# Attention's edge units scaled block by block, the next mLSTM head's decay made within the present head, fillers moved

## The chip, the cores and the metric

One Trainium2 chip, of which the program uses one core. The metric is device time in microseconds (us) of one execution, and the median of three executions is given. Names of engines: PE multiplies matrices (PEld loads its weights), DVE is the vector engine, ACT the scalar engine with the table functions, POOL the general engine (GpSimd), SP issues most DMA transfers.

## The reference

One decoder layer on 512 tokens of width 1024. A normalized input goes through one wide projection; two branches follow, an mLSTM matrix memory (4 heads of 256) and a sparse attention (8 query heads of 64 in 2 groups, with a compressed, a selected and a window part); gates merge them, and an output projection, the residual and a last norm follow. Cut to what is touched:

```python
hN = _rmsnorm(x, norm_g[l])
p = _split_in(hN @ w_in[l])
# mLSTM, one chunk: gates as cumulated decays, then a normalized product
logD = a[..., :, None] - a[..., None, :] + li[..., None, :]
m_t = jnp.maximum(inter, jnp.max(logD, axis=-1))
s = jnp.einsum('bhld,bhsd->bhls', qc, kc) * jnp.exp(logD - m_t[..., None])
h = num / jnp.maximum(jnp.abs(den), jnp.exp(-m_t))[..., None]
mh = _head_layernorm(mh, mh_norm_g[l]).astype(x.dtype)
# attention: softmax parts, each weighted by a gate per head and token
p_s = jax.nn.softmax(s_s, axis=-1)
p_w = jax.nn.softmax(jnp.where(m_w, s_w, NEG), axis=-1)
return g[..., 0:1] * o_c + g[..., 1:2] * o_s + g[..., 2:3] * o_w
# end
x = x + merged @ w_out[l]
return _rmsnorm(x, final_norm_g)
```

With 512 tokens in 8 selectable blocks of 64 and a window of 512, the selected and the window part both see every earlier token.

## The kernel before

Every large product is done in float32 by three passes: each operand is split into a high part (rounded) and a low rest, and high by high, high by low and low by high are added in PSUM. The split of a weight tile `wr` (128 x 1024) is one ACT copy to `wh` and one DVE subtraction to `wl`.

**Fillers.** The projection's columns, 128 at a time, are jobs of a `Stream` (line 164). `stream.step(n)` issues n of its matmuls (128 x 512, `pp<-hTh,wh` and the like) into the program; when a job is through, its `post` function evacuates it. The kernel places such steps by hand, by constants, between the parts of attention and of the mLSTM heads, so that PE has work while another engine prepares what it needs next. PE keeps the order that a scheduler makes of the program by its dependencies; ACT and DVE keep program order only while their name is in the set `ordered` (lines 68 to 82).

**Attention** consists of 16 units `(c, hh, b)`: four query pairs, two halves, two branches (selected and window). A unit has four query blocks `qb` of 128 rows, the causal part of each being 128, 256, 384 or 512 columns wide, all in one tile `P` (128 x 1280). `score` (line 1033) makes the scores of a block into PSUM `ps` (two buffers, tag `ps`), `softmax_block` (line 1024) takes the row's minimum of the negated scores with a custom DVE instruction (`P,st<-ps,cst`) and the exponential with its row sum on ACT. At the last block the reciprocals of the four sums and the gates are multiplied on DVE (`st`), and four POOL instructions (line 1055) scale P. `ptrans` (line 1057) then transposes P by PE (`pt<-cst,P`), and the products with the values follow (`po<-pth,vsw`). Scores run a unit ahead of the values. `tick` (line 1090) issues FILL = 3 filler steps between these pieces, in the last quarter two; between the four scores of the first unit it is START_FILL = 12. The compressed part (`sc`, `mx`, `pc`) runs beside it as a generator. Before attention stand the keys (`keys`), the compressed keys and values (`compress_k` writes `KC`, `compress_v` writes `VC`) and the first queries (`query_heads`, which turns them by position, `rope_b`, and splits them into `Th`); 4 and 14 filler steps lie between them (lines 967 to 972).

**mLSTM.** For each of four heads (loop at line 1255): the decay matrix `Dm` (a PE product of `sel` and `ghl` in PSUM, `dg` on DVE, seven exponentials on ACT), four score blocks times Dm, four value products into `num` with statistics (`bs`, `mv`) on DVE, then `rho` (the normalizer) and, over the power on POOL (`rlr`), the scale of each row, by which `num` is multiplied, on DVE for two of four blocks and on ACT for two. Transposes of num follow (`pt<-cst,num`). Each head's queries and keys (`qkh`, `qkl`) come from convolutions (`conv`, line 1178: three DVE steps `u<-pp,prm,u`, a tanh and a split) that are the `post` of filler jobs; before the transposes the loop steps the stream until the next head's last convolution is through (line 1324), in the last head NORM_FILL = 30 steps.

**Tail.** The last norm of row blocks 0 and 1: `more` and `factor` (lines 1457 and 1461) add up partial sums of squares `fb` and take the power `fr` on POOL, `last_factor` reduces the last piece by a custom DVE instruction, `times` and `both` multiply by the norm's weights, `scaled` multiplies by `fr` on ACT and stores.

Of the kernel before, what the change touches and what calls it, by code (L numbers as in the profile page):

```python
# [15 lines left out]
OP = mybir.AluOpType  # L16
# [4 lines left out]
NT = T // 128  # L21
ND = D // 128
# [1 line left out]
BIG = 1e30  # L24
NEGINF = -3.0e38
FILL = 3
START_FILL = 12
LAG = 1
BEHIND = 2
YIELDS = 6  # L30
NORM_FILL = 30

MQ, MK, MV, MO, MZ, MI = 0, 1024, 2048, 3072, 4096, 5120
NQ, NKC, NVC, NKS, NVS, NKW, NVW = 5128, 5640, 5768, 5896, 6024, 6152, 6280
# [26 lines left out]
def build(  # L61
# [5 lines left out]
    ordered = {"act", "dve"}  # L67
# [809 lines left out]

        cols(NQ + c * 128, post)

    def query_heads(c):  # L880
        raw, rot, a = roped.pop(("q", c))
        q = rope_b(raw, rot, a)
        Th = []
        for hh in range(2):
            s = slice(hh * 64, hh * 64 + 64)
            o = slice((1 - hh) * 64, (1 - hh) * 64 + 64)
            t = rpp.tile([128, T], F32R, name="Th", tag=f"Th{hh}")
            A(t[s, :], q[s, :], AF.Copy)
            dve.tensor_tensor(t[o, :], q[s, :], f(t[s, :]), OP.subtract)
            Th.append(t)  # L890
        heads[c] = raw, Th
# [71 lines left out]
    stream.run()  # L963
    keys(0, rope_b(*roped.pop(("k", 0))))
    u1 = hidden(1)
    stream.run()
    keys(1, rope_b(*roped.pop(("k", 1))))
    stream.step(4)
    ordered.update(("act", "dve"))
    query_heads(0)  # L970
    compress_k(u0)
    stream.step(14)
    compress_v(u1)
    ordered.clear()
    cmp_pool.__exit__(None, None, None)

# [47 lines left out]
    def softmax_block(c, hh, b, qb, pss, P, st):  # L1024
# [5 lines left out]
        )  # L1030
        A(pv, pv, AF.Exp, bias=st[:, 0, qb : qb + 1], scale=-1.0, accum_out=st[:, 1, qb : qb + 1])

    def score(c, hh, b, qb, pair):
        kh, kl = KK[c // 2]
        n = (qb + 1) * 128
        tq = heads[c][1][hh][:, qb * 128 : qb * 128 + 128]
        if qb == 0:
            if b == 0:
                pss = PS()
                pe.matmul(pss[:, :256], tq, kh[:, :, :128], start=True, stop=False)  # L1040
                pe.matmul(pss[:, :256], tq, kl[:, :, :128], start=False, stop=True)
                for i in range(2):
                    softmax_block(c, hh, i, 0, pss[:, i * 128 : i * 128 + 128], *pair[i])
            return
        pss = PS()
        pe.matmul(pss[:, :n], tq, kh[:, b, :n], start=True, stop=False)
        pe.matmul(pss[:, :n], tq, kl[:, b, :n], start=False, stop=True)
        P, st = pair[b]
        softmax_block(c, hh, b, qb, pss[:, :n], P, st)
        if qb == NT - 1:  # L1050
            dve.reciprocal(st[:, 2], st[:, 1])
            dve.tensor_tensor(st[:, 2], st[:, 2], gates[:, :, (2 * c + hh) * 3 + 1 + b], OP.mult)
            for j in range(NT):
                pj = P[:, POFF[j] : POFF[j] + (j + 1) * 128]
                pool.tensor_scalar(pj, pj, st[:, 2, j : j + 1], 1.0, OP.mult, OP.mult)  # L1055
# [187 lines left out]

        stream.add(load, gen)

    for h in range(4):
        for i in range(2):
            for e in range(2):
                conv(i, h, e)
    for j in range(ND):  # L1250
        branch(GB, j, ybh, ybl, 4)
    stream.run(4)
    values(0)

    for h in range(4):
        (qh, ql), (kh, kl) = qk[0, h], qk[1, h]
        vh, vl = vv[h]
        pgb = PS()
        sl = sel[:, h : h + 1].broadcast_to([128, 128])
        pe.matmul(pgb, sl, ghl, start=True, stop=True)  # L1260
# [6 lines left out]
        for sb in range(NT):  # L1267
            o, n = KOFF[sb], 512 - sb * 128
            bias = cs[:, sb, h : h + 1]
            A(Dm[:, o : o + 128], dg[:, sb * 128 : sb * 128 + 128], AF.Exp, bias=bias, scale=-1.0)  # L1270
            if n > 128:
                A(Dm[:, o + 128 : o + n], pgb[:, (sb + 1) * 128 :], AF.Exp, bias=bias, scale=-1.0)
        Sh = mp.tile([128, 1280], F32R, name="Sh", tag="Sh")
        Sl = mp.tile([128, 1280], F32R, name="Sl", tag="Sl")
        for sb in range(NT):
# [14 lines left out]
        for tb in range(NT):  # L1290
            po = PO() if tb == 2 else PT()
            for sb in range(tb + 1):
                a = KOFF[sb] + (tb - sb) * 128
                lh, ll = Sh[:, a : a + 128], Sl[:, a : a + 128]
                pe.matmul(po[:, :258], lh, vh[:, sb, :], start=sb == 0, stop=False)
                pe.matmul(po[:, :256], lh, vl[:, sb, :], start=False, stop=False)
                pe.matmul(po[:, :258], ll, vh[:, sb, :], start=False, stop=sb == tb)
            A(num[:, tb], po[:, :258], AF.Copy)
            dve.bn_stats(bs[:, tb], num[:, tb, 0:256])
            dve.bn_aggr(mv[:, tb], bs[:, tb])  # L1300
# [21 lines left out]
        if h < 3:  # L1322
            values(h + 1)
            while (1, h + 1, 1) not in ready:
                stream.step(1)
        else:
            stream.step(NORM_FILL)
        for e in range(2):
# [15 lines left out]
    with tc.tile_pool(name="fin", bufs=1, reuse_waits="tile") as fp:  # L1344
# [109 lines left out]
        def begin(tb):  # L1454
            keep(pool.tensor_scalar(fb[:, tb : tb + 1], fs[:, tb, 0:1], EPS, None, OP.add))

        def more(tb, n):
            v = fb[:, tb : tb + 1]
            keep(pool.tensor_tensor(v, v, fs[:, tb, n : n + 1], OP.add))

        def factor(tb, n):
            more(tb, n)
            keep(pool.tensor_tensor(fr[:, tb : tb + 1], fb[:, tb : tb + 1], mhalf[:, 0:1], OP.pow))  # L1463

        def last_factor(tb, cs, n):
# [96 lines left out]
        product((None, Y[1]), "MS4", w3, False, tbs=(1,), cs=halves_of[0])  # L1562
        join(1, R0, Y[1][:, halves_of[0]])
        square(1, R0, 1)
        times(0, R)
        factor(0, 1)
        more(1, 1)
        scaled(0, L)
        scaled(0, R)
        product((None, Y[2]), "MS4", w3, False, tbs=(1,), cs=halves_of[1])  # L1570
# [27 lines left out]
```

## Time and profile before

| | us |
|---|---|
| median of 3 runs (lowest to highest) | 612.02 (611.96 to 612.77) |
| the profiled execution | 612.24 |
| its span, from first to last instruction | 610.4 |

The granted clock is 0.997. What is quoted from the profile further on has these forms. A row of the page's first part is an engine's busy time, its share of the span and the count of its instructions. A wait row names engine and tile that waited, the engine and tile that released it, then total us, times and longest. A row of stretches is "start:end length", then the busy time and count of PE, PEld, DVE, ACT and POOL, the granted clock, the DMA share and GB/s. A timeline row is start, duration, engine, line, operation, output and inputs with shapes, count, and in brackets the idle time ahead of it and what ended it. A row of groups is line, engine, operation, tiles, shapes and count, then the summed time in us and the mean in ns, then idle time. L77 is the line of the helper that records most instructions, so the tiles tell them apart.

### The profile page before, as it was taken

The numbers are of one execution on the slowest core, as the hardware profiler recorded it, in microseconds if no ns is written. First come the engines' busy times: TensorE is split into PE (matmuls) and PEld (weight loads), VectorE is DVE, ScalarE is ACT, GpSimd is POOL, SyncE is SP. The second block draws the span as 40 slices with busy tenths as digits, with TensorE's granted clock in tenths as the row PEclk, the third lists the DMA queues.
The fourth block names the chain that finished last, engine by engine and source line by source line (L and its number), as shares of the span: only waits on it lengthen the run. The fifth ranks groups of instructions, "written<-read, shape, count | busy, mean of one in ns | idle before, by whom it ended". The sixth has DMA issues, their size and how long they took to land. (4 is left out here: it accounts for less than half of the span.)

```text
span 610.4 us, 8577 instructions
## 1 busy us (share of the span) xinstructions
PE 596.2 (98%) x3008; PEld 499.5 (82%) x3008; DVE 483.1 (79%) x906; ACT 343.2 (56%) x635; POOL 63.4 (10%) x126
## 2 busy tenths in 40 slices
PE   8999999999999999999999999999999999999995
PEld 6988888888888877888888887888788878888884
DVE  5879798696686578886977684889898997589984
ACT  6854646664442356665765674465756563434564
POOL 3000000000100003222122131000000000010122
PEclk9999999999999999999999999999999999999998
DMA  7966555302068361323313113422242234890633
GB/s 221 349 162 190 183 168 160 116 2 86 18 185 207 78 173 46 97 59 86 81 47 103 53 34 122 138 70 70 69 130 80 89 87 131 301 253 18 208 52 139
DMA packets 83637, 74.18 MB, mean 122 GB/s; under 512 B 5197, under 2 KB 65225, under 8 KB 83594
## 3 DMA queue, kind: packets, MB, share of 16 engines
q1 hardware_dynamic: 82296, 70.94, 39.1%
q0 software_dynamic: 1008, 2.36, 2.1%
q8 instruction: 24, 0.39, 0.3%
q10 hardware_dynamic: 290, 0.33, 0.2%
q14 instruction: 19, 0.16, 0.1%
HBM read 61.36 MB, written 8.45 MB: 114 GB/s over the span
## 5 line engine op out<-in xcount | busy, mean ns | idle before, releaser
L77 PE MATMUL pp<-hTh,wh 128*128 128x512 f32 (+1 forms) x360 | 143.8, 400 | 0.0
L77 PE MATMUL pp<-hTl,wh 128*128 128x512 f32 (+1 forms) x360 | 139.9, 389 | 0.0
L77 PE MATMUL pp<-hTh,wl 128*128 128x512 f32 (+1 forms) x360 | 139.5, 388 | 0.0
L77 ACT ACTIVATE wh<-wr 128x1024 fp32r<-128x1024 f32 x56 | 59.1, 1060 | 50.5 <-PE pp L77 44.6
L77 DVE TENSOR_TENSOR wl<-wr,wh 128x1024 fp32r<-128x1024 f32 x56 | 68.2, 1219 | 21.1 <-ACT wh L77 21.0
L77 PEld LDWEIGHTS pp<-hTh,wl 128*128 128x128 f32 x360 | 67.7, 188 | 13.1
L77 PEld LDWEIGHTS pp<-hTh,wh 128*128 128x128 f32 x360 | 67.9, 189 | 10.7
L77 PEld LDWEIGHTS pp<-hTl,wh 128*128 128x128 f32 x360 | 68.0, 189 | 9.4
L1055 POOL TENSOR_SCALAR P<-P,st 128x128 f32<-128x128 f32 (+1 forms) x64 | 38.1, 615 | 152.5 <-DVE st L77 134.4
L77 ACT ACTIVATE P<-P,st 128x128 f32<-128x128 f32 (+3 forms) x64 | 35.7, 558 | 22.1 <-DVE st L77 21.2
L77 DVE TENSOR_TENSOR ptl<-pt,pth 128x512 fp32r<-128x512 f32 (+1 forms) x64 | 30.9, 486 | 16.2 <-ACT pth L77 15.0
L77 DVE TENSOR_TENSOR wl<-T,wh 128x1024 fp32r<-128x1024 f32 x28 | 33.9, 1221 | 11.4 <-ACT wh L77 11.3
L77 DVE TENSOR_TENSOR wl<-R,wh 128x1024 fp32r<-128x1024 f32 x28 | 33.8, 1219 | 9.5 <-ACT wh L77 9.5
L77 ACT ACTIVATE wh<-T 128x1024 fp32r<-128x1024 f32 x28 | 29.4, 1057 | 18.4 <-PE pp L77 10.3
L77 ACT ACTIVATE pth<-pt 128x512 fp32r<-128x512 f32 (+1 forms) x64 | 27.2, 426 | 18.8 <-PE pt L77 18.4
L77 ACT ACTIVATE wh<-R 128x1024 fp32r<-128x1024 f32 x28 | 29.1, 1057 | 13.8 <-PE pp L77 6.7
L77 DVE SCALAR_TENSOR_TENSOR u<-pp,prm,u 128x511 f32<-128x511 f32 (+2 forms) x48 | 35.6, 742 | 0.4 <-ACT u L77 0.2
L77 DVE CUSTOM_DVE_ANT_0 P<-ps,cst 128x128 f32<-128x128 f32 (+3 forms) x64 | 30.5, 483 | 5.0 <-PE ps L77 4.8
L77 PE MATMUL pt<-cst,P 128*128 128x128 f32 x160 | 29.6, 275 | 2.7 <-POOL P L1055 2.5
L77 PE MATMUL ps<-k,Th 128*128 128x256 f32 (+2 forms) x112 | 29.0, 339 | 0.2 <-DVE st L77 0.2
L77 PEld LDWEIGHTS pt<-cst,P 128*128 128x128 f32 x160 | 20.7, 141 | 10.2 <-POOL P L1055 4.7
L77 PE MATMUL pp<-yah,wh 128*128 128x512 f32 x64 | 25.0, 391 | 0.0
(345 smaller groups left out, 1341.4 us busy)
## 6 DMA issues: line engine op xcount, KB each, us to landing
wr<-w_in SPq DMA_DIRECT2D x44, 512.0 KB
R<-w_in SPq DMA_DIRECT2D x24, 512.0 KB
gD<-sg SPq DMA_DIRECT2D x16, 256.0 KB
s<-gD SPq DMA_DIRECT2D x16, 256.0 KB
wr<-w_branch_a SPq DMA_DIRECT2D x8, 512.0 KB
R<-w_out SPq DMA_DIRECT2D x8, 512.0 KB
vD<-cq SPq DMA_DIRECT2D x8, 256.0 KB
wr<-vD SPq DMA_DIRECT2D x4, 512.0 KB
```

Of the source, the lines that this page charges most:

```text
L77: ins = fn(*args, **kw)
L1055: pool.tensor_scalar(pj, pj, st[:, 2, j : j + 1], 1.0, OP.mult, OP.mult)
```

## The change

The first unit and the last are scaled per block: as soon as a block has its row sum, a reciprocal is taken on DVE, and one instruction multiplies the block by that reciprocal and by the gate; on POOL for the first three blocks, on DVE for the fourth, in a piece of 128 columns and one of 384. The compressed keys and values are made and evacuated earlier, the first queries are turned before the four fillers, 20 steps stand ahead of attention instead of 14, and 7 between the first scores instead of 12. The decay of a head is a function, called for the next head after the last value product of the present one; the first is made between two filler jobs. Four filler steps are added after the next head's convolutions, and 36 instead of 30 stand in the last head. In the tail two sums of `more` are made on DVE, the first ahead of `times`.

```diff
-START_FILL = 12
+START_FILL = 7
+PRE_FILL = 20
+EDGES = (0, 15)
...
-NORM_FILL = 30
+NORM_FILL = 36
+NEXT_FILL = 4
...
-    def query_heads(c):
+    def query_turned(c):
         raw, rot, a = roped.pop(("q", c))
-        q = rope_b(raw, rot, a)
+        return raw, rope_b(raw, rot, a)
+
+    def query_heads(c, turned=None):
+        raw, q = turned or query_turned(c)
...
     u1 = hidden(1)
+    compress_k(u0)
     stream.run()
     keys(1, rope_b(*roped.pop(("k", 1))))
+    compress_v(u1)
+    ordered.update(("act", "dve"))
+    first = query_turned(0)
     stream.step(4)
-    ordered.update(("act", "dve"))
-    query_heads(0)
-    compress_k(u0)
-    stream.step(14)
-    compress_v(u1)
+    query_heads(0, first)
+    stream.step(PRE_FILL)
     ordered.clear()
...
+    def block_scaled(c, hh, b, qb, P, st):
+        g = (2 * c + hh) * 3 + 1 + b
+        r, gate_of = st[:, 2, qb : qb + 1], gates[:, qb, g : g + 1]
+        dve.reciprocal(r, st[:, 1, qb : qb + 1])
+        cut = 128 if qb == NT - 1 else 0
+        pj = P[:, POFF[qb] : POFF[qb] + (qb + 1) * 128]
+        for eng, part in ((dve, pj[:, :cut]), (dve if cut else pool, pj[:, cut:])):
+            if part.shape[1]:
+                eng.tensor_scalar(part, part, r, gate_of, OP.mult, OP.mult)
...
-        if qb == NT - 1:
+        if units.index((c, hh, b)) in EDGES:
+            for j in (0, 1) if qb == 1 else (qb,):
+                block_scaled(c, hh, b, j, P, st)
+        elif qb == NT - 1:
             dve.reciprocal(st[:, 2], st[:, 1])
...
+    decayed = {}
+
+    def decay(h):
         pgb = PS()
...
+        decayed[h] = Dm
...
-    stream.run(4)
+    stream.run(2)
+    decay(0)
+    stream.run(2)
     values(0)
...
+        Dm = decayed.pop(h)
...
+            if tb == 3 and h < 3:
+                decay(h + 1)
             A(num[:, tb], po[:, :258], AF.Copy)
...
                 stream.step(1)
+            stream.step(NEXT_FILL)
         else:
             stream.step(NORM_FILL)
...
-        def more(tb, n):
+        def more(tb, n, eng=None):
             v = fb[:, tb : tb + 1]
-            keep(pool.tensor_tensor(v, v, fs[:, tb, n : n + 1], OP.add))
-
-        def factor(tb, n):
-            more(tb, n)
+            keep((eng or pool).tensor_tensor(v, v, fs[:, tb, n : n + 1], OP.add))
+
+        def factor(tb, n, eng=None):
+            more(tb, n, eng)
...
+        factor(0, 1, dve)
         times(0, R)
-        factor(0, 1)
-        more(1, 1)
+        more(1, 1, dve)
```

Three places show what stands in a row now. The first is DVE at the end of the first unit's scores, before; `ISA P,st<-ps,cst` is the custom instruction of a score block, `ISA st` its row result, `sc` and `mx` belong to the compressed part, `wl` is a weight split:

```order
L77 ISA P,st<-ps,cst 128x512
L77 ISA st 128x1
L77 TENSOR_TENSOR mx<-mx,gates 128x8
L77 TENSOR_TENSOR sc<-sc,mx 128x256
L77 ISA P,st<-ps,cst 128x256
L77 ISA st 128x1
L77 TENSOR_TENSOR sc<-sc,cst 128x256
L77 RECIPROCAL st<-st 128x4
L77 ISA P,st<-ps,cst 128x384
L77 ISA st 128x1
L77 TENSOR_TENSOR st<-st,gates 128x4
L77 TENSOR_TENSOR wl<-wr,wh 128x1024
```

The same place of the same engine, from the reciprocal of the 512-column block to its two pieces, with the change:

```order
L80 RECIPROCAL st<-st 128x1
L80 TENSOR_TENSOR wl<-wr,wh 128x1024
L80 TENSOR_REDUCE mx<-sc 128x8
L80 ISA P,st<-ps,cst 128x256
L80 ISA st 128x1
L80 RECIPROCAL mx<-mx 128x8
L80 RECIPROCAL st<-st 128x1
L80 ISA P,st<-ps,cst 128x384
L80 ISA st 128x1
L80 TENSOR_TENSOR mx<-mx,gates 128x8
L80 TENSOR_SCALAR P<-P,st,gates 128x128
L80 TENSOR_TENSOR sc<-sc,mx 128x256
```

The weight split has moved ahead of the scaling of the fourth block, and so have two score blocks of the next unit.

The second place is PE in the last two units' transposes (`pt<-cst,P`) and value products (`po`), before; `pp<-` rows are fillers:

```order
L77 MATMUL po<-pth,vsw 128x384
L77 MATMUL po<-ptl,vsw 128x384
L77 MATMUL pt<-cst,P 128x128
L77 MATMUL po<-pth,vsw 128x256
L77 MATMUL po<-ptl,vsw 128x256
L77 MATMUL pt<-cst,P 128x128 x2
L77 MATMUL po<-pth,vsw 128x128
L77 MATMUL pt<-cst,P 128x128
L77 MATMUL pp<-hTh,wh 128x512
L77 MATMUL pt<-cst,P 128x128
L77 MATMUL pp<-hTl,wh 128x512
L77 MATMUL po<-ptl,vsw 128x128
```

The same products with the change:

```order
L80 MATMUL pp<-hTh,wl 128x512
L80 MATMUL pp<-hTh,wh 128x512
L80 MATMUL po<-ptl,vsw 128x384
L80 MATMUL pt<-cst,P 128x128
L80 MATMUL po<-pth,vsw 128x256
L80 MATMUL pp<-hTl,wh 128x512
L80 MATMUL pp<-hTh,wl 128x512
L80 MATMUL po<-ptl,vsw 128x256
L80 MATMUL pt<-cst,P 128x128 x4
L80 MATMUL po<-pth,vsw 128x128
L80 MATMUL pp<-hTh,wh 128x512
L80 MATMUL po<-ptl,vsw 128x128
```

Fillers now stand ahead of the four transposes of the last unit, which follow one another.

The third place is ACT at the end of head 1 of the mLSTM, before; `num` is the copy of a value product or its scaling, `vh` the high part of the next head's values, `rho` the normalizer, `th`, `u` and `qkh` belong to a convolution:

```order
L77 ACTIVATE num<-po 128x258
L77 ACTIVATE num<-pt 128x258
L77 ACTIVATE vh<-wr 128x4x256
L77 ACTIVATE rho<-num 128x4
L77 ACTIVATE th<-u 128x512
L77 ACTIVATE qkh_4357<-u 128x512
L77 ACTIVATE wh<-wr 128x1024
```

And with the change:

```order
L80 ACTIVATE num<-pt 128x258
L80 ACTIVATE vh<-wr 128x4x256
L80 ACTIVATE th<-u 128x512
L80 ACTIVATE Dm<-dg,cs 128x128
L80 ACTIVATE Dm<-ps,cs 128x384
L80 ACTIVATE Dm<-dg,cs 128x128
L80 ACTIVATE Dm<-ps,cs 128x256
L80 ACTIVATE Dm<-dg,cs 128x128
L80 ACTIVATE Dm<-ps,cs 128x128
L80 ACTIVATE qkh_4363<-u 128x512
L80 ACTIVATE Dm<-dg,cs 128x128
L80 ACTIVATE rho<-num 128x4
```

The seven exponentials of the next head's decay now stand between the last copy of num and rho.

More of the change, by code (lines that the diff above doesn't have):

```diff
@@ L1244, in branch @@
         stream.add(load, gen)
[L1246 to L1251, printed above, removed]
-    stream.run(4)
[L1253 to L1257, printed above, removed]
+    decayed = {}
+    def decay(h):
         pgb = PS()
@@ L1272, in build @@
                 A(Dm[:, o + 128 : o + n], pgb[:, (sb + 1) * 128 :], AF.Exp, bias=bias, scale=-1.0)
+        decayed[h] = Dm
+    for h in range(4):
+        for i in range(2):
+            for e in range(2):
+                conv(i, h, e)
+    for j in range(ND):
+        branch(GB, j, ybh, ybl, 4)
+    stream.run(2)
+    decay(0)
+    stream.run(2)
+    values(0)
+    for h in range(4):
+        (qh, ql), (kh, kl) = qk[0, h], qk[1, h]
+        vh, vl = vv[h]
+        Dm = decayed.pop(h)
         Sh = mp.tile([128, 1280], F32R, name="Sh", tag="Sh")
```

## The prediction

> **What bounds the kernel.** I read the page first, then what the matrix engine (PE) waits for, then its stretches, then the timeline at each wait.
>
> ```profile
> PE 596.2 (98%) x3008; PEld 499.5 (82%) x3008; DVE 483.1 (79%) x906; ACT 343.2 (56%) x635; POOL 63.4 (10%) x126
> PEclk9999999999999999999999999999999999999998
> PE pt L77 <- POOL P L1055: 2.5, 5, 1.0
> PE pt L77 <- DVE num L77: 1.1, 2, 0.6
> PE pp L77 <- DVE KC L77: 0.4, 1, 0.4
> PE ps L77 <- ACT qkh L77: 0.3, 1, 0.3
> PE ps L77 <- DVE st L77: 0.2, 1, 0.2
> 219.00:233.00 14.00, 12.13 (x60) 8.90 (x59) 11.92 (x38) 9.24 (x27) 2.52 (x4) 1.00 0.39 111
> 352.00:371.00 19.00, 17.46 (x95) 13.81 (x94) 13.74 (x41) 11.92 (x32) 8.27 (x12) 1.00 0.27 81
> 437.00:460.00 23.00, 22.50 (x122) 19.28 (x121) 22.25 (x51) 14.45 (x26) 1.16 (x3) 1.00 0.31 92
> 460.00:490.00 30.00, 29.89 (x156) 25.26 (x154) 27.58 (x58) 17.46 (x35) 1.15 (x3) 1.00 0.29 88
> ```
>
> PE is busy 98% of the span, at full clock. The change leaves its matmuls as they are, so it can only win the time in which PE stands still. The wait rows (total, times, longest) name five such places, all of them touched by the change. The stretch rows (length, then busy time of PE, weight load, DVE, ACT, POOL) show them to be two stretches of attention, its first and last unit, and the mLSTM heads, where DVE is nearly full.
>
> A busy time hides part of a gap, because a matmul's end is modelled. So I count from start to start.
>
> ```profile
> 219.45 0.39 PE L77 MATMUL pp<-hTh,wl 128*128 128x512 f32 x1
> 220.24 0.55 PE L77 MATMUL pp<-KC,rh 128*128 128x64 f32 x3 [0.40 <-DVE KC L77]
> ...
> 224.29 0.48 PE L77 MATMUL ps<-k,Th 128*128 128x256 f32 x2 [0.24 <-DVE st L77]
> ...
> 230.07 0.60 PE L77 MATMUL pp<-cst,sc 128*64 128x128 f32 x4
> ...
> 231.66 0.33 PE L77 MATMUL pt<-cst,P 128*128 128x128 f32 x1 [0.99 <-POOL P L1055]
> ...
> 458.50 0.39 PE L77 MATMUL pp<-hTh,wh 128*128 128x512 f32 x1
> 458.73 0.39 PE L77 MATMUL pp<-hTl,wh 128*128 128x512 f32 x1
> ...
> 459.61 0.30 PE L77 MATMUL pt<-cst,num 128*128 128x128 f32 x1 [0.50 <-DVE num L77]
> ```
>
> A filler matmul with another behind it takes 0.23 us (458.50 to 458.73; 0.227 over many). In the first unit PE therefore lost 220.24 − 219.45 − 0.23 = 0.56, then 0.41 ahead of the scores at 224.29. Four small matmuls of about 0.11 each end at 230.5, and the transpose starts at 231.66, a loss of 1.15. Two more gaps behind it, of 0.15 and 0.45, make **2.7 us**. The same count gives **2.9** in the last unit, in seven gaps of which the largest, 0.85, ends at 368.02 (its row is below). In the heads it gives 0.24, 0.42, 0.66 (458.73 to 459.61, less 0.23) and 0.73 at 489.5, together **2.05**. All of it is 7.65 us; the tail comes on top.
>
> **First unit.** Before, the four softmax blocks are scaled together on POOL once the last block's row sums are there; now each is scaled as soon as it has its own, and the last one on DVE.
>
> ```profile
> 227.60 0.64 DVE L77 CUSTOM_DVE_ANT_0 P<-ps,cst 128x512 f32<-128x512 f32 x1
> ...
> 228.28 0.73 ACT L77 ACTIVATE P<-P,st 128x512 f32<-128x512 f32 x1
> ...
> 228.91 0.18 ACT L77 ACTIVATION_READ_ACCUMULATOR P<-P,st 128x1 f32 x1
> ...
> 230.14 1.22 DVE L77 TENSOR_TENSOR wl<-wr,wh 128x1024 fp32r<-128x1024 f32 x1
> ...
> 230.48 2.81 POOL L1055 TENSOR_SCALAR P<-P,st 128x128 f32<-128x128 f32 x4 [51.39 <-DVE st L77]
> L77 DVE RECIPROCAL st<-st 128x4 f32<-128x4 f32 x16 | 2.8, 176 | 5.9 <-ACT P L77 5.8
> L77 DVE TENSOR_SCALAR num<-num,rho 128x256 f32<-128x256 f32 x8 | 2.5, 348 | 0.1
> ```
>
> The sums are complete at 229.09, but POOL starts at 230.48 and needs 2.81 us for all four. The three small blocks leave this path. On it remain, from the start of the custom instruction: 0.64 and 0.85 (sums 1.49 behind it), 0.18 for a reciprocal, then what stands on DVE ahead of the first 128-column piece. The order gives one wl split (1.22), a reduction and some small steps of the compressed softmax (about 0.9), the score reductions of two blocks of the next unit (about 1.1), and the piece itself. No row shows a DVE scaling by two operands of 128 columns: nearest is 0.35 for 256 by one, so it lies between 0.17 (the reciprocal, hardly any data) and 0.35; I take 0.25. Neighbours overlap by some 0.07 each (DVE's rows at 603.05 and 603.66 in the tail do), 0.6 in all: 1.49 + 0.18 + 1.22 + 0.9 + 1.1 + 0.25 − 0.6 + 0.25 from score to custom instruction = 4.8. PE meanwhile has 13 fillers (2.95) and other scores and transposes for 1.36, hence 4.3: **0.5 stays**, without the overlaps 1.1. Three scores ahead of that wait for two PSUM buffers, which a wl split on DVE frees late: 0 to 0.6, I take 0.3. The KC copies leave the queue behind the long Th splits (0.56 goes), with 0.4 kept for the later transposes and for weights that are split later than before. Together 1.2 stays of 2.7: gain **1.5** (0.5 to 2.5).
>
> **Last unit.**
>
> ```profile
> 366.51 1.22 DVE L77 TENSOR_TENSOR wl<-wr,wh 128x1024 fp32r<-128x1024 f32 x1
> ...
> 368.02 0.78 PE L77 MATMUL pt<-cst,P 128*128 128x128 f32 x2 [0.69 <-POOL P L1055]
> ...
> L1055 POOL TENSOR_SCALAR P<-P,st 128x128 f32<-128x128 f32 x1 | 1.2, 1180 | 4.8 <-PE po L77 4.8
> ...
> L1055 POOL TENSOR_SCALAR P<-P,st 128x128 f32<-128x128 f32 x1 | 0.4, 372 | 7.5 <-DVE st L77 7.5
> ```
>
> The last two rows are POOL alone, grouped over 366.7 to 368 and over 352 to 353. Here PE has no fillers left and follows POOL block by block. The counts say what changes: 4 × (12 − 7) = 20 fillers fewer between the first scores, 20 − 14 = 6 more ahead of them, so 14 × 0.227 = 3.2 us of PE work is still there at the end, and the order puts it between these transposes. That is more than the 2.9 lost. The first three blocks are also scaled earlier, and the fourth no longer queues on POOL. DVE's price is four reciprocals and two pieces, about 1.3, less the two small ones before, in a stretch where it is busy 13.74 of 19: hidden. One transpose next to few fillers may still wait: **0.3 stays**, gain 2.6 (1.5 to 2.9).
>
> The first 128-column block took 1.18 us beside the wl split, and 0.37 with DVE elsewhere. The Trainium skill, "SBUF — State Buffer", section "Who interferes with whom", says that a DVE instruction with two SBUF inputs and a POOL instruction that reads SBUF exclude each other for a whole instruction; the trace agrees (three times 0.37 beside a split of 1.22). It speaks against this change in so far as blocks now begin at four times instead of one, each of which can fall on a split; the price is the second rival's.
>
> **mLSTM heads.** The decay of head h+1 (one PE product, dg on DVE, seven exponentials on ACT) moves ahead of the norm of head h; four fillers follow the last convolution.
>
> ```profile
> L77 DVE TENSOR_TENSOR dg<-ps,cst 128x512 f32<-128x512 f32 x4 | 2.7, 681 | 0.1
> ...
> L77 ACT ACTIVATE Dm<-dg,cs 128x128 f32<-128x128 f32 x16 | 6.3, 393 | 0.6 <-DVE dg L77 0.6
> L77 ACT ACTIVATE Dm<-ps,cs 128x384 f32<-128x384 f32 x4 | 2.2, 562 | 0.0
> ...
> L77 ACT ACTIVATE Dm<-ps,cs 128x256 f32<-128x256 f32 x4 | 1.8, 460 | 0.0
> ...
> L77 ACT ACTIVATE Dm<-ps,cs 128x128 f32<-128x128 f32 x4 | 1.4, 358 | 0.0
> ```
>
> The two score waits (0.24 and 0.42) go: qkh no longer stands between those exponentials. The norm gets something in front instead. On ACT rho now follows (6.3 + 2.2 + 1.8 + 1.4) / 4 = 2.93 us of exponentials, on DVE dg costs 0.68. Walking heads 1 and 2 by the new order, DVE has its own splits and convolution steps until about the time at which rho arrives (idle 0 to 0.6), and 1.1 us less work stands between the last statistics and the scaling. But PE also has fewer fillers there, 44 instead of 47 and 45. So 0.68 + 0.3 − 1.1 + 0.4 = 0.3 more or 0.9 less (four fillers, if convolution work and not the norm is late) than the 0.7 of now: I take **0.5 in each of the two heads**, and none in head 0 (60 fillers for 54, DVE work up alike) or head 3. Gain 2.05 − 1.0 = **1.05** (−1 to 2.05).
>
> **Tail.**
>
> ```profile
> 603.05 0.69 DVE L77 TENSOR_TENSOR xo<-xo,late 128x512 f32<-128x512 f32 x1 [0.46 <-ACT junk L77]
> 603.10 0.69 POOL L1459 TENSOR_TENSOR fb<-fb,fs 128x1 f32<-128x1 f32 x1 [2.22 <-ACT junk L77]
> ...
> 603.66 0.42 DVE L77 SCALAR_TENSOR_TENSOR xo<-pp,xo 128x256 f32<-128x256 f32 x1
> 603.87 0.55 POOL L1463 TENSOR_TENSOR fr<-fb,prm 128x1 f32<-128x1 f32 x1
> ...
> 604.61 0.48 DVE L77 CUSTOM_DVE_ANT_0 junk<-xo,fb 128x256 f32<-128x256 f32 x1 [0.53 <-POOL fb L1459]
> ```
>
> The last reduction, at 604.61, waits for POOL's second sum (fb), which queues behind its first and the power (fr, to 604.42). On DVE both sums cost about 0.17 each (a reciprocal's size); then times, join and reduction follow without POOL: 603.05 + 0.17 + 0.61 + 0.17 + 0.35 = 604.35. Gain **0.3** (0 to 0.5), straight into the end.
>
> **Sum.** 1.5 + 2.6 + 1.05 + 0.3 = 5.45. The profiled execution took 612.24 (span 610.4, 1.84 around it), 0.2 above the median of 612.02: 612.24 − 5.45 = **606.8 us**. With every stall and 0.5 of the tail gone: 612.24 − 8.15 = 604.1.
>
> **Rivals.**
> 1. *Nearly all goes*, 604.1 to 605.2: if DVE reaches the pieces and the norm in time. Against it speaks DVE's 22.25 of 23 us. 0.10.
> 2. *POOL is blocked by splits*: each block that meets one costs 1.18 − 0.37 = 0.81. If two in each unit do and their transposes come next, 3.2 us come back: 610.0; with one in each, 608.4. For it: 2.81 us for four blocks now. Against: the new blocks have microseconds of lead. By the skill's page just named it is possible at every split. With a first unit that gains nothing (608.3) this is 608.2 to 610.8, 0.17.
> 3. *The fillers only change place*: 3.2 us fewer at the start, where per-block scaling saves just 1.2 because DVE is late. The start loses 2.0, the end gains 2.6, the tail 0.3, the heads nothing: 611.3, no difference that can be told. 0.07.
> 4. *Slower*: DVE stops at rho in the heads. If it stands for all of dg and the exponentials, 3.6 us, less 0.9 of fillers, the transposes are 2.7 later in each of three heads, 8.1 in all, beside losses that remain: 612.24 − 4.4 + 8.1 = 615.9. It turns the sign once the heads lose 5.6, or 1.9 each: DVE idle 2.8 us at rho. For it: at 460 to 490 DVE has only 2.4 us free in 30. Against: a vl split, a u step and a qkl step stand in front of rho in the new order. 0.05.
>
> **Numbers.** Forecast 0.61 (605.2 to 608.2), rivals 0.10, 0.17, 0.07, 0.05. A measurement tells 0.2% (1.2 us) from no change. Faster: 0.61 + 0.10 + 0.17 = 0.88; same 0.07; slower 0.05. The range 604.4 to 609.8 leaves out part of rival 1, the end of 2, and 3 and 4, about 0.2.
>
> **What would show it.** Waits of PE for POOL should fall from 2.5 to under 0.5, and a wait for P on DVE near the start be about 0.5. PE from 352 to 371 should lose under 0.5. KC and qkh should be gone from its waits, num stay at about 0.7 in sum by the wait rows. The last reduction should stand about 5.45 ahead of where it was, 0.3 of it by the tail's own change. It is wrong if DVE shows over 1 us of idle time before rho in a head, if POOL blocks of about 1.2 us stand ahead of a waiting transpose, or if weights come late between 203 and 221, where their splits are moved behind the rotated queries.

## The result, and the profile after

| | before | after |
|---|---|---|
| median (lowest to highest), us | 612.32 (611.96 to 612.77) | 608.1 (607.9 to 609.29) |
| ratio to before, 95% interval | | 0.9932 (0.992 to 0.9944) |
| span of the profiled execution, us | 610.4 | 606.2 |

The kernel before has a fourth run here, hence 612.32 instead of 612.02. The change wins 0.7%, about 4.2 us. Forecast were 606.8 (604.4 to 609.8), so the sign and the range held, and a quarter of the forecast gain is missing. In the spans the sum comes out as 610.4 − 606.2 = 4.2 instead of 5.45.

First the page's engine row of the changed kernel:

```profile
PE 594.8 (98%) x3008; PEld 500.0 (82%) x3008; DVE 485.7 (80%) x916; ACT 343.8 (57%) x635; POOL 65.9 (11%) x122
```

Then what PE waits for, without the waits of the first 20 us (total, times, longest):

```profile
PE pt L80 <- DVE num L80: 1.9, 2, 1.0
PE po L80 <- DVE ptl L80: 0.8, 2, 0.6
```

And the stretches that answer to the four shown of before, which lie 2 to 3 us earlier now (length, then busy time of PE, PEld, DVE, ACT, POOL):

```profile
216.00:231.00 15.00, 15.00 (x82) 12.53 (x80) 12.41 (x44) 9.77 (x28) 2.84 (x4) 1.00 0.49 141
350.00:369.00 19.00, 19.00 (x106) 15.50 (x104) 13.99 (x35) 11.38 (x28) 3.26 (x6) 1.00 0.36 104
435.00:458.00 23.00, 22.06 (x122) 18.75 (x122) 21.63 (x49) 15.37 (x31) 2.06 (x3) 1.00 0.31 92
458.00:488.00 30.00, 29.04 (x150) 24.49 (x149) 27.68 (x59) 18.51 (x36) 2.05 (x3) 1.00 0.29 88
```

PE is busy all the time in both edge stretches, where 12.13 of 14 and 17.46 of 19 were busy before, and no wait of PE for POOL is left. But the wait for num has grown from 1.1 to 1.9, POOL is busy about 2.06 instead of 1.16 in the heads' stretches, and a wait stands there that was not there before: for `ptl`, the low part of transposed P.

To see it as a sum, PE's lost time is counted from start to start, over all 3008 matmuls, against the pace of their width (0.227 us for 512 columns, 0.175 for 384, 0.118 for 256, 0.108 for 128), by stretches of the span. The first 20 us are the arrival of the input, which differs by up to 1.1 between runs and is left out of the comparisons that follow. "Tail" is from the last matmul's start to the end. The prediction counted named gaps alone (2.7, 2.9 and 2.05); the table counts every small difference in a stretch too, so its losses are larger, and gains are what can be compared.

| PE's lost time, us | first 20 | first unit (200 to 234) | inside attention (to 350) | last units (to 374) | heads (to 520) | tail |
|---|---|---|---|---|---|---|
| before | 4.86 | 3.81 | 2.05 | 3.71 | 3.73 | 7.29 |
| after | 4.62 | 0.73 | 3.81 | 1.01 | 4.06 | 7.09 |
| gain | 0.24 | 3.08 | −1.76 | 2.70 | −0.33 | 0.20 |

The edges gave 5.8 and the tail 0.2. Attention between its edges took 1.8 back, which no step of the prediction had, and the heads took 0.3 where a gain of 1.05 was forecast.

Where the heads wait now, in the changed kernel's timeline of head 1, by DVE, POOL and PE (start, duration, what it is, idle time ahead of it):

```profile
451.46 0.16 DVE L80 TENSOR_SCALAR va<-va 128x4 f32<-128x4 f32 x1
451.53 1.22 DVE L80 TENSOR_TENSOR wl<-wr,wh 128x1024 fp32r<-128x1024 f32 x1
453.65 0.16 DVE L80 TENSOR_TENSOR rlt<-va,rlr 128x4 f32<-128x4 f32 x1 [0.91 <-POOL rlr L125]
...
451.70 1.92 POOL L125 TENSOR_TENSOR rlr<-va,prm 128x4 f32<-128x4 f32 x1 [6.88 <-DVE va L80]
...
454.35 0.39 PE L80 MATMUL pp<-hTh,wl 128*128 128x512 f32 x1
455.68 0.30 PE L80 MATMUL pt<-cst,num 128*128 128x128 f32 x1 [0.94 <-DVE num L80]
```

The power of four numbers per row took 1.01 at this place in the kernel before:

```profile
456.60 1.01 POOL L122 TENSOR_TENSOR rlr<-va,prm 128x4 f32<-128x4 f32 x1 [7.87 <-DVE va L77]
```

It takes 1.92 here. It was issued 0.17 after a weight split on DVE, and it ends 0.87 after that split. In heads 0 and 3, where no split is under way when it starts, the power still takes 1.04 and 1.01. In head 0 a split of two SBUF operands does follow, 0.54 behind the power's start, and neither is longer for it (the power took 1.04 in head 0 of the kernel before, with nothing on DVE beside it; a qkl split takes 0.69 in head 1 too):

```profile
420.32 1.04 POOL L125 TENSOR_TENSOR rlr<-va,prm 128x4 f32<-128x4 f32 x1 [9.78 <-DVE va L80]
...
420.86 0.69 DVE L80 TENSOR_TENSOR qkl<-u,qkh 128x512 fp32r<-128x512 f32 x1
```

In head 1 DVE then waits 0.91 for it, and PE stands for 455.68 − 454.35 − 0.23 = 1.10.

Inside attention, the same timeline near the largest new gap:

```profile
242.35 1.24 DVE L80 TENSOR_TENSOR wl<-wr,wh 128x1024 fp32r<-128x1024 f32 x1
...
243.62 2.06 DVE L80 TENSOR_TENSOR Th<-ra,Th 64x512 fp32r<-64x512 f32 x2
...
246.05 0.41 DVE L80 TENSOR_TENSOR ptl<-pt,pth 128x256 fp32r<-128x256 f32 x1
...
246.52 0.39 PE L80 MATMUL po<-ptl,vsw 128*128 128x256 f32 x1 [0.60 <-DVE ptl L80]
...
241.39 3.75 POOL L1075 TENSOR_SCALAR P<-P,st 128x128 f32<-128x128 f32 x4 [7.66 <-DVE st L80]
```

PE waits for a ptl that stands on DVE behind a weight split and both splits of the second query pair's Th. Those two take 2.06 beside POOL's scaling, while in the kernel before they stood apart and took 0.69 each. POOL's four blocks take 3.75 here and took 2.23 in the corresponding unit before:

```profile
241.38 0.69 DVE L77 TENSOR_TENSOR Th<-ra,Th 64x512 fp32r<-64x512 f32 x1
...
246.46 0.69 DVE L77 TENSOR_TENSOR Th<-ra,Th 64x512 fp32r<-64x512 f32 x1
...
249.18 2.23 POOL L1055 TENSOR_SCALAR P<-P,st 128x128 f32<-128x128 f32 x4 [9.39 <-DVE st L77]
```

Each engine is longer at its work beside the other.

### The profile page after: what moved, and what is told of

It is laid out like the page before. It is cut to its first block, busy times and chain, and to the rows that moved or that the text cites. A ratio compares the mean times of both kernels' runs of the same rounds, so it can differ in the third digit from the quotient of the medians.

```text
span 606.2 us, 8569 instructions
## 1 busy us (share of the span) xinstructions
PE 594.8 (98%) x3008; PEld 500.0 (82%) x3008; DVE 485.7 (80%) x916; ACT 343.8 (57%) x635; POOL 65.9 (11%) x122
## 4 chain that ended last, share of the span: by engine, by line
PE 89%; DVE 4%; ACT 3%; issue 1%; POOL 1%; DMA 1%; SPq 0%; POOLq 0%; DVEq 0%; ACTq 0%
PE pp L80 53%; PE ps L80 20%; PE pt L80 12%; PE po L80 4%; DVE wl L80 1%; DMA xt<-x 1%; POOL rlr L125 1%; DVE xo L80 1%; ACT Dm L80 1%; DVE u L80 1%; ACT wh L80 1%; POOL fr L1494 0%; DVE Th L80 0%; ACT xo L80 0%; ACT qkh L80 0%
## 5 line engine op out<-in xcount | busy, mean ns | idle before, releaser
L80 PE MATMUL pp<-hTl,wh 128*128 128x512 f32 (+1 forms) x360 | 143.8, 399 | 0.0
L80 PE MATMUL pp<-hTh,wh 128*128 128x512 f32 (+1 forms) x360 | 140.4, 390 | 0.0
L80 DVE TENSOR_TENSOR wl<-wr,wh 128x1024 fp32r<-128x1024 f32 x56 | 69.7, 1246 | 12.6 <-ACT wh L80 12.4
L1075 POOL TENSOR_SCALAR P<-P,st 128x128 f32<-128x128 f32 (+3 forms) x56 | 35.1, 646 | 96.0 <-DVE st L80 73.6
L80 PE MATMUL pt<-cst,P 128*128 128x128 f32 x160 | 28.3, 273 | 0.0
```

The costliest lines, as they stand in the source:

```text
L80: ins = fn(*args, **kw)
```

## The experiments

Two questions were open. In the heads: does the norm come late because the next decay stands in front of it (**queue theory**, the prediction's fourth rival in a small form), or because POOL's power meets a weight split (**blocking theory**, the second rival's mechanism in another place)? In attention: do the 14 fillers that were moved make the new losses, or the scaling by blocks? Each kernel's lost time is counted as in the table above. Runs 2 and 9 were timed ten and four times; the others are one execution each and are read by lost time in a stretch, because the first 20 us alone differ by up to 1.1. Beside runs 1 to 4 the kernel before took 612.65 (median of 13), beside runs 5 to 8 611.76 (one execution), beside runs 9 to 11 612.26 (median of 7).

**1. Attention's part alone.** The changed kernel, with the heads and the tail as before:

```diff
-NORM_FILL = 36
-NEXT_FILL = 4
+NORM_FILL = 30
...
-    stream.run(2)
-    decay(0)
-    stream.run(2)
+    stream.run(4)
...
+        decay(h)
         Dm = decayed.pop(h)
...
-            if tb == 3 and h < 3:
-                decay(h + 1)
...
-            stream.step(NEXT_FILL)
...
-        factor(0, 1, dve)
         times(0, R)
-        more(1, 1, dve)
+        factor(0, 1)
+        more(1, 1)
```

> The attention part of the change alone (per-block scaling of the first and last unit, early compressed keys and values, fillers moved); the heads and the tail as before. If the parts are independent, PE's lost time between 200 and 380 us falls by about 4.0 as in the changed kernel (5.9 won at the edges, 1.9 lost between them) and the heads lose 3.7 as before: span about 606.4. If the attention part owes its gain to the heads' part or pays for it, the span is off this by over 0.5.

Span 606.8, one time of 608.56. Lost: 0.73 in the first unit, 3.82 inside attention, 1.01 in the last units, 3.83 in the heads, and a tail of 7.31. The span is 0.4 over the forecast, of which 5.24 − 4.86 = 0.38 lies in the first 20 us. The parts are independent as far as one execution tells, and this part alone brings practically all that the whole change brings.

**2. The heads' part alone.** The kernel before, with the decay made ahead and the fillers after the convolutions:

```diff
-NORM_FILL = 30
+NORM_FILL = 36
+NEXT_FILL = 4
...
-    stream.run(4)
+    stream.run(2)
+    decay(0)
+    stream.run(2)
...
+            if tb == 3 and h < 3:
+                decay(h + 1)
...
+            stream.step(NEXT_FILL)
```

> The heads' part alone (decay of the next head in the present one, four fillers after the convolutions, 36 in the last head); attention and tail as before. By both theories the two waits for num stay near 1.1 each and the span is 610.4 to 610.9, no faster than before. Blocking theory: the power on POOL takes about 1.9 in heads 1 and 2, where a wl split stands behind it on DVE. Queue theory: the power's duration does not matter, the chain is late before it.

613.07 against 612.65 (ratio 1.0008, 0.9999 to 1.0018): no gain. The profiled span was 611.8, over the forecast by 0.9, which is what the first 20 us took more (5.75 for 4.86). The heads lose 4.13, the power takes 1.92 and 1.91 in heads 1 and 2, and the two waits are 1.11 and 1.13. So the loss belongs to this part and not to anything in attention.

**3. Six fillers instead of four.** One number of the changed kernel:

```diff
-NEXT_FILL = 4
+NEXT_FILL = 6
```

> The changed kernel with 6 instead of 4 fillers after the convolutions. In the order this puts a convolution step (one input in PSUM) instead of the wl split behind the norm's last va on DVE in heads 1 and 2, and leaves 42 instead of 44 fillers ahead of the first transpose. Blocking theory: the power on POOL takes 1.0 instead of 1.9, the waits of PE for num fall from 1.1 to under 0.5 each, span about 604.7. Queue theory (dg and the seven exponentials ahead of rho make the chain late): the chain is as late as before and PE comes 0.45 earlier, so each wait grows to about 1.5, span about 607.0.

PE's waits of this kernel hold one for num:

```profile
PE pt L80 <- ACT num L80: 0.4, 2, 0.2
```

Its timeline shows POOL's power and its neighbours on DVE in head 1:

```profile
451.73 0.16 DVE L80 TENSOR_SCALAR va<-va 128x4 f32<-128x4 f32 x1
451.85 0.75 DVE L80 SCALAR_TENSOR_TENSOR u<-pp,prm,u 128x510 f32<-128x510 f32 x1
453.01 0.16 DVE L80 TENSOR_TENSOR rlt<-va,rlr 128x4 f32<-128x4 f32 x1 [0.42 <-POOL rlr L125]
...
451.97 1.01 POOL L125 TENSOR_TENSOR rlr<-va,prm 128x4 f32<-128x4 f32 x1 [5.57 <-DVE va L80]
```

The power takes 1.01 again beside a convolution step, which reads one operand from PSUM. The gaps ahead of the transposes fall from 1.10 and 1.12 to 0.38 and 0.37, though PE reaches them with two fillers fewer, and the heads lose 3.12 instead of 4.06. That is what the blocking theory said; the queue theory wanted 1.5 each. But the edit moved other steps as well: counted from the head's last value product, the power also starts 1.3 sooner than in the changed kernel, and a weight split now stands behind it in the chain, so the scaling of num starts 1.2 sooner in all (the table of the heads further on). The drop is therefore not the price of the blocked power alone. The span, 606.1, is less telling, since the first 20 us took 0.77 more than in the changed kernel; without these, 601.6 falls to 600.7, by 0.9 where 1.5 was expected.

**4. The decay back in its own head,** the added fillers kept:

```diff
+        if h:
+            decay(h)
         Dm = decayed.pop(h)
...
-            if tb == 3 and h < 3:
-                decay(h + 1)
```

> The changed kernel with the decay of heads 1 to 3 made at the start of their own head again; all else stays, the added fillers too. In the order a wl split stands behind va in head 2, a convolution step in head 1. Queue theory: both waits for num fall under 0.4, and waits of the scores for qkh return (0.4 to 0.7). Blocking theory: the wait in head 1 falls, and in head 2 the power takes 1.9 again and the wait stays near 1.

In the timeline of this kernel, the power beside a convolution step (head 1) and beside a split (head 2) of the same execution:

```profile
452.75 1.01 POOL L125 TENSOR_TENSOR rlr<-va,prm 128x4 f32<-128x4 f32 x1 [6.55 <-DVE va L80]
481.57 1.95 POOL L125 TENSOR_TENSOR rlr<-va,prm 128x4 f32<-128x4 f32 x1 [4.24 <-DVE va L80]
```

And PE's waits there:

```profile
PE ps L80 <- ACT qkh L80: 0.6, 1, 0.6
PE pt L80 <- DVE num L80: 0.5, 2, 0.4
```

The power follows the blocking theory to the letter. The waits follow neither: 0.54 in head 1, and 0.33 with another 0.27 in head 2, less than 1 although the power was held up. Both things count then: without the decay in front the power starts sooner in head 2 (4.8 after the last value product, where the changed kernel has 7.5), and being held up costs less. In exchange the scores wait for qkh again (0.74 from start to start). In sum the heads lose 3.97, as much as with the decay moved.

**5. The fillers back, the scaling kept:**

```diff
-START_FILL = 7
-PRE_FILL = 20
+START_FILL = 12
+PRE_FILL = 14
```

> The changed kernel with the fillers around the first scores as before (14 and 12), the per-block scaling of both edge units kept. Theory that the fillers' move makes the new losses inside attention: the stream is then where it was, the two splits of Th stand apart again in the order, the wait of 0.77 near 245 goes, and PE loses about 1.3 between 240 and 340 as before instead of 3.0. Theory that the per-block scaling makes them: 3.0 stays. In the last unit the fillers run out: 1 to 2 us are lost there, the first unit loses under 0.5. Span about 606.0 by the first theory, 607.5 by the second.

PE's waits of this kernel hold one in attention:

```profile
PE pt L80 <- POOL P L1075: 0.4, 1, 0.4
```

Its timeline has the two Th splits apart again:

```profile
237.52 0.96 DVE L80 TENSOR_TENSOR Th<-ra,Th 64x512 fp32r<-64x512 f32 x1 [0.36 <-ACT Th L80]
...
241.35 0.69 DVE L80 TENSOR_TENSOR Th<-ra,Th 64x512 fp32r<-64x512 f32 x1
```

The wait near 245 is gone, and inside attention PE loses 2.34 instead of 3.81: moving the fillers made that loss, by shifting which job falls beside which unit. The last units lose 1.39, just 0.4 more than with the fillers kept for them, and the first unit 0.64. Span 605.5, time 607.34 beside 611.76. By the total of one execution this could not be told from the whole change (0.9928 of the kernel before, and 0.9932); by the lost time between 200 and 374 it is 1.2 better (4.37 for 5.55), so of the change's parts the fillers' move was better left out.

**6. No unit scaled by blocks, the fillers moved:**

```diff
-EDGES = (0, 15)
+EDGES = ()
```

> The changed kernel with no unit scaled per block; the fillers stay moved. If the scaling is what saves the first unit, PE loses 2.7 there as before and up to 3.2 more, as it has 14 fillers fewer: 3 to 6 between 200 and 240 instead of 0.9. If the last unit is saved by the fillers alone, it stays under 0.7 lost between 360 and 380; if it needs the scaling too, 1.5 or more. By the fillers' theory the losses of 3.0 between 240 and 340 stay. Span 608.5 to 611.

PE's waits of this kernel:

```profile
PE pt L80 <- POOL P L1075: 2.6, 3, 1.3
```

The wait for POOL is back at its old size. The first unit loses 2.69 and the last units 2.97; time 612.26 beside 611.76. The fillers alone take 0.74 off the end (3.71 to 2.97), the scaling with the old fillers 2.3 (3.71 to 1.39). The middle loses 3.33, so most of its loss comes with the moved fillers, as their theory has it. But the wait of 0.77 near 246 is missing here, so that one needs both the moved fillers and the scaling by blocks; the later ones for `ptl` (0.39 and 0.27) are there. The first unit lost less than forecast, 2.69 for 3.81 before: its transposes still wait, but the gaps of 0.56 (KC) and 0.41 (ahead of the scores) are gone, and the 14 missing fillers cost nothing that shows. The early KC copies and turned queries are in this run and in run 5; no run takes them out, so their share of the first unit's gain is not known by itself.

**7. Two numbers together.** Fewer fillers moved, more after the convolutions:

```diff
-PRE_FILL = 20
+PRE_FILL = 26
-NEXT_FILL = 4
+NEXT_FILL = 8
```

> The changed kernel with 26 instead of 20 fillers ahead of attention and 8 instead of 4 after the convolutions. In the order both splits of the second query pair's Th then stand ahead of the unit's scaling on POOL instead of beside it. Blocking theory: the splits take 1.4 together instead of 2.06, the wait near 245 goes, and the power takes 1.0; the last unit keeps 8 of the 14 fillers (1.8 us) and loses up to 1.2. Span 603.5 to 605.5. If the queue alone makes the wait, it stays at about 0.8 and the span is about 605.5 or more.

Span 605.9, time 607.7. The timeline shows the two splits ahead of POOL's scaling, which starts at 245.41:

```profile
242.44 1.40 DVE L80 TENSOR_TENSOR Th<-ra,Th 64x512 fp32r<-64x512 f32 x2
```

They take 1.40, the power takes 1.01, the last units lose 1.18 and the wait near 245 has gone, all as the blocking theory said. But another wait of 0.50 ends at 303.58; 2.77 are lost inside attention. The heads lose 3.76, with gaps of 0.75 and 0.74 ahead of the transposes. The span is 0.4 over the forecast. The first 20 us took 0.85 more than in the changed kernel, and what the heads lost the next run explains.

**8. Eight fillers after the convolutions alone:**

```diff
-NEXT_FILL = 4
+NEXT_FILL = 8
```

> The changed kernel with 8 fillers after the convolutions. In the order 45 fillers stand ahead of the first transpose of heads 1 and 2 instead of 42 with 6, the convolution step stays behind va. If what is left of the waits for num with 6 fillers (0.38 and 0.37) is just lateness, 3 more fillers (0.68) take it away: heads lose 0.7 less than there, span 605.4 with the same start. If other waits take its place, 606.1 stays.

The timeline of head 1, with POOL's power, the end of the norm on DVE and PE's transposes:

```profile
452.12 1.01 POOL L125 TENSOR_TENSOR rlr<-va,prm 128x4 f32<-128x4 f32 x1 [5.57 <-DVE va L80]
...
455.54 0.16 DVE L80 TENSOR_TENSOR rho<-rho,rlr 128x4 f32<-128x4 f32 x1
455.65 1.23 DVE L80 TENSOR_TENSOR wl<-wr,wh 128x1024 fp32r<-128x1024 f32 x1
456.79 0.61 DVE L80 TENSOR_SCALAR num<-num,rho 128x256 f32<-128x256 f32 x2
...
457.29 0.52 PE L80 MATMUL pt<-cst,num 128*128 128x128 f32 x3 [0.59 <-DVE num L80]
```

The power is not blocked, and PE waits all the same, 0.75 in each of two heads. With 8 fillers the scheduler sets a weight split (1.23) between rho and the scaling of num, which with 6 it had set earlier, between two other steps of the norm (453.12 in run 3). More cover did not help, because the order filled it with the next split. Span 606.5; the expectation of 605.4 was a miss.

**9. Both cures.** Fillers as in run 5, six after the convolutions as in run 3:

```diff
-START_FILL = 7
-PRE_FILL = 20
+START_FILL = 12
+PRE_FILL = 14
-NEXT_FILL = 4
+NEXT_FILL = 6
```

> Both cures together: fillers around the first scores as before (14 and 12) and 6 after the convolutions, the rest of the change kept. If the two are independent, PE loses 2.3 inside attention instead of 3.8, 1.4 instead of 1.0 in the last unit and 3.1 instead of 4.1 in the heads: 2.0 less than the changed kernel, time about 606.1, ratio to the kernel before about 0.990. If the stream's other place changes the order in the heads, the gain in the heads is missing: about 607.1.

606.33 against 612.26, ratio 0.9903 (0.9886 to 0.9919). Lost: 0.65, 2.30, 1.38, 3.14 by the four stretches, as forecast. It beats both kernels: the change's 0.9932 lies above this interval.

**10. The same with ten after the convolutions** (`NEXT_FILL = 10`).

> The same with 10 instead of 6 fillers after the convolutions. In the order DVE then stands idle through the power in heads 1 and 2 (nothing between va and the next step), but a wl split stands between rho and the scaling of num. If lateness alone counts, 4 more fillers (0.9) cover what is left, and the heads lose 2.4. If the place of the split in the row counts, as the run with 8 suggests, the wait for num is 0.3 to 0.8 in each of the two heads and the heads lose 3.1 to 3.8.

606.36. The heads lose 3.08, and no gap of over 0.1 is left ahead of the transposes, though a split stands between rho and the scaling as in run 8. More cover is not the reason: between the last value product and the first transpose PE has 9.88 us of matmuls here and in run 9 alike. The scheduler has instead set `rho` on ACT ahead of the seven exponentials, where it stood behind them in run 9:

```profile
446.98 0.20 ACT L80 ACTIVATE rho<-num 128x4 f32<-128x4 f32 x1
447.22 0.41 ACT L80 ACTIVATE Dm<-dg,cs 128x128 f32<-128x128 f32 x1
```

The power then starts 1.5 sooner, DVE stands idle 1.13 through the power, and the scaling is through before PE comes to it. The 0.75 of run 8 are not there, but a gap of 0.4 between two fillers near 491 (for `mB`, which takes up a branch's product) and smaller ones are, so the sum is that of run 9. Neither of the two expectations fits: the four fillers changed the order, on ACT as on DVE, and not the cover.

**11. No moved decay, eight after the convolutions,** fillers as in run 5:

```diff
-START_FILL = 7
-PRE_FILL = 20
+START_FILL = 12
+PRE_FILL = 14
...
-NEXT_FILL = 4
+NEXT_FILL = 8
...
+        if h:
+            decay(h)
         Dm = decayed.pop(h)
...
-            if tb == 3 and h < 3:
-                decay(h + 1)
```

> Fillers around the first scores as before, 8 after the convolutions, and the decay of heads 1 to 3 at the start of their own head. In the order no wl split stands beside the power in heads 1 and 2 nor between rho and the scaling. If the moved decay is worth something, the scores' waits for qkh come back (0.4 to 0.7) and the heads lose 3.5 or more. If the fillers after the convolutions are what helps, the heads lose 3.1 or less without it.

607.85. The heads lose 4.79. The power takes 1.01 in both heads, but PE waits 0.91 and 1.02 for ACT's num, in head 1 behind qkh in ACT's row, and the scores wait for qkh (0.71 from start to start). So the moved decay is worth something once its norm is not held up, and fillers alone don't replace it. How much is not settled by one pair of runs: 4.79 − 3.1 = 1.7 against runs 9 and 10, which have other numbers of fillers, and 4.79 − 3.76 = 1.0 against run 7, which has eight but other fillers in attention.

## Why the prediction was right or wrong, point by point

**What bounds the kernel: right.** The time went where PE stood still, and PE's work did not change (3008 matmuls in both kernels). The gain of the stretches adds up: 0.24 + 3.08 − 1.76 + 2.70 − 0.33 + 0.20 = 4.13 of 4.2 in the span.

**First unit: right in kind, too small.** 1.2 was to stay of 2.7. No gap of the named ones stayed. The step that failed is the sum of 4.8 from the custom instruction to the 128-column piece. It set the exponential (0.85) ahead of the weight split, because the first reciprocal in the order was taken for that of the 512-column block. It is that of the 384-column block (the text ahead of the second order listing has the same mistake). The split therefore ran beside the exponential, as the changed kernel's timeline shows:

```profile
222.99 2.22 POOL L1048 TENSOR_SCALAR P<-P,st,gates 128x256 f32<-128x256 f32 x2 [0.45 <-DVE st L80]
...
222.81 0.67 DVE L80 CUSTOM_DVE_ANT_0 P<-ps,cst 128x512 f32<-128x512 f32 x1
...
223.48 1.20 DVE L80 TENSOR_TENSOR wl<-wr,wh 128x1024 fp32r<-128x1024 f32 x1
...
225.96 0.33 DVE L80 TENSOR_SCALAR P<-P,st,gates 128x128 f32<-128x128 f32 x1
...
226.72 0.27 PE L80 MATMUL pt<-cst,P 128*128 128x128 f32 x1
```

From 222.81 the piece was done at 226.29, 3.5 later and not 4.55, and PE took it 0.4 after, without a wait. The piece itself, bounded by 0.17 and 0.35 and taken at 0.25, took 0.33.

**Last unit: right in size, wrong in cause.** 2.6 was forecast and 2.70 measured. The prediction put it in the main on the 14 fillers, so the size came out right in part by luck; runs 5 and 6 show that the scaling by blocks gives 2.3 by itself and the fillers 0.74 by themselves.

**The fillers' price: missed.** The prediction counted the 14 fillers as work that waits at the end and asked what the start loses by them (the third rival, which did not come: the start lost nothing). It did not ask what else the stream carries. Each job ends in a post on ACT and DVE, and queries, splits and rotations then fall beside other units. Attention lost 1.76 more between its edges; run 5, with the fillers back, regains 1.47, and run 6, with the fillers moved and no scaling by blocks, loses 1.28 more than the kernel before.

**Heads: the step that failed is the walk of the norm.** It gave 0.5 of wait in each of two heads; 1.10 and 1.12 were measured. It left the power at its old 1.01, although the order showed a weight split right behind va. The traces of head 1, counted from the start of its last value product, show what that took (us):

| head 1 | rho on ACT | power starts | it takes | DVE scales num from | PE's matmuls until the transposes | wait |
|---|---|---|---|---|---|---|
| before | 1.55 | 8.44 | 1.01 | 10.96 | 10.79 | 0.66 |
| after | 4.83 | 7.46 | 1.92 | 10.93 | 10.33 | 1.10 |
| run 3, six fillers | 4.31 | 6.14 | 1.01 | 9.76 | 9.88 | 0.38 |
| run 8, eight fillers | 4.31 | 6.14 | 1.01 | 10.81 | 10.56 | 0.75 |
| run 10, ten fillers, attention's as before | 1.77 | 4.68 | 1.01 | 8.85 | 9.88 | 0 |

Though rho came 3.3 later on ACT, the power started 1.0 sooner than before, so the walk's terms for what stands in front (0.68 + 0.3 − 1.1, nearly nothing) were too careful. What the sum lacked is the longer power: it took 0.9 back, the scaling came as late as before, and the wait grew by 0.44, the two fillers that PE has fewer there (the sum's 0.4). In head 2 the power started 0.5 sooner, ended 0.4 later, and the wait grew by those 0.4. That does not make the decay in front free: in run 10, where rho goes ahead of it, the power starts another 1.5 sooner than in run 3, though other steps on DVE stand elsewhere there too.

The prediction quoted a rule that bears on this, the Trainium skill's "SBUF — State Buffer", section "Who interferes with whom", and weighed it for the softmax blocks alone. In all twelve other kernels and this one the power takes 1.91 to 1.95 when a split of two SBUF operands began 0.14 to 0.17 ahead of it, and 1.01 to 1.04 beside a step with an operand in PSUM or beside no step. As the prediction put it, exclusion for a whole instruction, the rule goes too far for the other order: the split in head 0 that began 0.54 behind the power overlapped it for 0.5 us and held nothing up.

**Tail: 0.20 for 0.3.** Counted from DVE's first step behind ACT's row sum (`times` before, the first sum now), the last reduction came after 600.17 − 598.98 = 1.19 instead of 604.61 − 603.05 = 1.56, a gain of 0.37, so 0.17 were lost behind it. The first power, now issued beside `times`, takes longer in the changed kernel's timeline:

```profile
599.05 0.68 DVE L80 TENSOR_TENSOR xo<-xo,late 128x512 f32<-128x512 f32 x1
...
599.21 0.93 POOL L1494 TENSOR_TENSOR fr<-fb,prm 128x1 f32<-128x1 f32 x1 [2.42 <-DVE fb L80]
...
600.18 1.95 ACT L80 ACTIVATE xo<-xo,fr 128x512 f32<-128x512 f32 x3 [0.83 <-POOL fr L1494]
```

It takes 0.93 for the 0.55 of before, with ACT's three scalings behind it. These now end last, at 602.13, where DVE's last multiplication ends at 602.08 (before it was DVE that ended last, at 606.51). So they explain 0.05 to 0.07 of the 0.17; the rest lies behind the last store's issue, and its cause is open.

**Rivals.** The first did not come, as the heads kept their waits. The second came in its mechanism, but its price fell in the heads. In its own place, the first unit, POOL's block of 384 columns did meet the weight split of 223.48: it took 1.56, where the block of that width in the last unit took 0.66. It ended at 225.21 (its row, merged with the block before it, is shown under the first unit), and PE came to these blocks at 225.23, so it cost nothing, by luck. The fourth was close in direction, as the heads did get slower, but DVE never stopped at rho for long.

**Signs.** The waits for POOL, KC and qkh went as named, and the wait for P on DVE that was to stay at the start did not come. The wait for num did not stay at 0.7 but rose to 1.9 by the wait rows, and the last reduction came 604.61 − 600.17 = 4.44 sooner instead of 5.45.

## What to carry to other kernels

A filler is not just matrix time: moving it moves the work that its job ends in, so its new neighbours on the other engines belong in the sum. Where a small POOL step is in a chain, look in the order at what DVE starts just ahead of it, since the difference here was 0.9 us for a step of 1.0. And when one part of a change already makes up for a wait (the scaling by blocks), try the other part (the fillers) out of it: both numbers here were better at other values, 0.9903 instead of 0.9932. Adding a few fillers also changes the order that the scheduler makes, so what a run with more of them shows is not only more cover.

## What the runs showed of the hardware

A POOL power that starts 0.14 to 0.17 behind a DVE subtraction of two SBUF operands does not slow down in proportion: in head 1 it ended 0.87 after the split's end (452.75 to 453.62), nearly a whole power later, as if it had begun only then. A split that starts 0.54 behind the power cost neither anything. It goes the other way too: two DVE splits of 0.69 took 2.06 together (0.96 and 1.07) beside POOL's scaling, and 1.40 in run 7, where they were through before it began. In run 6 they began 0.09 ahead of POOL and took 1.46, and POOL's first two blocks took 0.83 and 0.91 there instead of 0.37 and 0.48. And the first 20 us of the span, in which PE waits for the input, vary by 1.1 us between runs of practically the same start (4.62 to 5.75), more than several of the parts weighed here.
